# S5 tables on VectorE, the loads of M on GpSimd's queue, and the first q and k weights ahead of the S5 inputs, in a two-layer hybrid trunk

## The chip, the cores and the metric

One core of one Trainium2 chip. The metric is the device time of one execution in microseconds (us). The kernel before took 1287.1 us in the median of three runs (1284.03, 1287.1 and 1289.07).

## What is computed

Two layers over 512 tokens of width 1024, all in float32. Each layer has a mixer and a channel mixer, and both are modulated per sequence by columns that come from a conditioning vector:

```
mod = silu(c) @ mod_w[l] + mod_b[l]            # shift1, scale1, gate1, shift2, scale2, gate2
h = x * (1 + scale1) + shift1
u, q, k, v = split(h @ w_in[l], 512 each)
ssm = s5_mixer(u)       # 32 groups, 16 channels in, 64 complex diagonal states, scan over the tokens, GELU, GLU
att = diff_attention(rotary(q), rotary(k), v)  # 4 heads, two causal softmax maps per head, RMS norm
x = layer_norm(alpha * x + (1 + gate1) * (concat(ssm, att) @ w_out[l]))
h = x * (1 + scale2) + shift2
x = layer_norm(alpha * x + (1 + gate2) * ((silu(h @ w_gate) * (h @ w_up)) @ w_down))
```

## The kernel before

**Products.** Every large product is made as three matmuls in a rounded float32 (mm3, L116): high part by high part, high by low and low by high. A weight tile (wunit) is one 512 KB transfer on SP's queue (wraw, L263), one copy on ScalarE that makes its high part (whi, L113), and one subtraction on VectorE for its low part (wlo, L104). Two wraw buffers and five of each part go round. L101, L104, L107 and L110 are helpers for VectorE (or GpSimd, where `eng` says so), L113 for ScalarE.

**S5.** The 32 groups are worked in four quarters q. For each quarter a layer needs tables. s5_build makes `Gt` and `QT` (two halves each; a half is three products or sums of 128x512: `o = a1*b1`, `ta = a2*b2`, `o = o -/+ ta`, in the inner function cpart), the matrix `kps` on TensorE, its copy `ksb`, and the store of that into a DRAM buffer `kd`. QT goes through TensorE (qps) and becomes Q. s5_rot makes the rotation tables `cs`, from `thl` (two products of 128x256), and stores them into the DRAM buffer `sC`. With these, a quarter runs: inp (UU is copied from u2, the rotation tables come back as `csl`), scan (vps on TensorE, rp and wz on VectorE, with the decay table `dt` that GpSimd writes, L575), and sout (yps from `M` and from Gt). M is eight transfers of 64 KB out of kd. One half of each Gt and QT, and both products of thl, are GpSimd's in the kernel before; the other halves are VectorE's. Layer 0 builds its tables inside its own mixer. Layer 1's are built during layer 0's channel mixer (build_bg), the last two quarters in its down projection, where layer 1's Gt, Q and cs are parked in DRAM.

**S5 inputs.** `us` are the four token blocks of u. s5_u2 spreads each over partitions by four transfers of 64 KB into u2 (16 in all per layer, shown as `u<-us`, L554).

**Order of the work.** After the first stage of layer 0 (u and half of v), the loop over the rest of v and over the q and k products of the four heads calls tick() after each few matmuls. A table of due times (PLAN) says at which tick the next step of the builds, of S5, of attention, of a weight's prefetch ('pf') or of a modulation column ('mod': a 512 KB load `mraw` and one pass of VectorE, L110) is emitted. A scheduler then sets the order inside each engine. Every engine and every DMA queue works its list in that order.

**Attention.** scores, transposed, values for 16 blocks (4 heads of 4), then per head scale (`es` by a power on GpSimd, then `on` = the head's output in PSUM times es, four activations on ScalarE, L791) and output (transposes of on, then `am`).

The end of the down projection's first half needs the gate row G2: it is copied by GpSimd's queue to DRAM and comes back as a broadcast (`G<-gd`), after a one-element copy on GpSimd (`after`, L330) that ties the buffer's reuse to earlier work.

Of the kernel before, what the change touches and what calls it, by code (L numbers as in the profile page):

```python
# [21 lines left out]
PLAN = ({'bld': [1.0733576, 2.9031205, 3.5154466, 12.5034164, 15.1071975, 15.6334384, 16.0575658, 21.8153328, 21.8163328, 22.2319658, 22.2329658, 28.5923397, 30.243001, 33.8382641, 37.0440198, 39.0572108, 39.0582108, 41.3108793, 50.0177884, 51.0998781], 's5': [4.9028951, 13.7411167, 15.9929821, 16.2119172, 16.2129172, 17.6168929, 28.8382807, 31.1407667, 34.4657886, 37.933134, 41.1334701, 41.8351188, 44.9709324, 49.1653528, 55.811875, 56.282631, 56.282731, 74.3701229, 75.0322375, 75.0323375], 'att': [32.001, 32.001001, 32.001002, 32.001003, 32.001004, 32.001005, 32.001006, 32.001007, 37.6865938, 41.7355913, 48.001, 48.2683932, 48.2683942, 48.2683952, 48.2683962, 48.2683972, 48.2683982, 48.617537, 61.3736509, 64.3309693, 65.5921236, 65.5931236, 65.5941236, 65.5941246, 65.5941256, 65.6288754, 65.6288764, 65.6288774, 72.5231302, 73.1266492, 78.0578164, 79.9687438, 81.2657271, 81.530476, 81.5768716, 81.5778716, 82.4637908, 82.4647908, 82.4657908, 83.044295, 83.5736498, 83.5746498, 83.5756498, 85.5723498, 85.6572802, 85.6582802, 85.6592802, 85.9764616, 85.9861658, 89.2215451, 89.674753, 89.674754, 93.4177513, 94.279308, 95.5776624, 99.2190776], 'mod': [13.3492705, 20.2546708, 27.3038673, 31.5542422, 38.8480964, 42.1955201, 43.0984851, 43.8754292, 43.8754302, 48.1035539, 49.3327831, 49.3327841, 49.5166057, 49.5176057, 49.5176067, 49.5176077, 59.8309932, 64.8347651, 77.2024317, 86.1901018], 'pf': [15.228123, 15.3414063, 23.4890323, 23.4900323, 40.4066783, 41.3304558, 48.9949729, 60.7543422, 71.3047183, 78.705196, 86.021538, 89.4349823, 89.827606, 96.6870796], 'cs': [0.6433489, 0.9702106, 4.3739515, 6.5989136]}, {'s5': [0, 13.9288025, 14.9687107, 23.4071258, 23.6099155, 23.9930522, 23.9930532, 23.9930542, 49.9536728, 50.7293131, 50.7303131, 52.6273113, 52.801288, 54.037998, 59.8058402, 63.0448533, 63.0448543, 63.0448553, 76.7900745, 79.030225], 'att': [32.001, 32.001001, 32.001002, 32.001003, 32.001004, 36.5544774, 36.5554774, 49.1404333, 49.1534776, 49.5360247, 49.5370247, 49.5380247, 49.9621102, 50.2217672, 52.4983559, 53.4634231, 53.4644231, 53.4654231, 55.4277196, 58.3250688, 61.5574297, 61.5584297, 61.5594297, 61.5604297, 64.4714996, 64.4715006, 64.4715016, 64.4715026, 64.4715036, 64.4715046, 64.4715056, 64.4715066, 64.4715076, 64.4715086, 64.4715096, 64.4715106, 64.4715116, 64.4715126, 80.4714996, 80.4715006, 80.4715016, 80.4715026, 81.6228446, 85.1505891, 85.1515891, 85.1525891, 87.7329811, 89.4506396, 89.4516396, 89.4526396, 89.4536396, 89.4546396, 92.1036248, 92.1036258, 95.1259822, 99.6815179], 'pf': [1.9638689, 9.1450603, 14.6524633, 14.6534633, 19.8486984, 32.001, 37.8876977, 48.001, 51.1731991, 74.7986995, 80.482311, 90.088235, 93.088235, 96.9]})  # L22
OPT = {'MQ': 'sync', 'MODQ': 'sync', 'q_bld': 1, 'q_s5': 0, 'q_att': 0, 'q_pf': 0, 'CSQ': 'scalar', 'plo': [[1, 0, 1, 0, 0, 0, 0, 0, 0, 0, 0, 0, 0, 0, 0, 0, 0, 0], [0, 0, 0, 0, 0, 0, 1, 1, 1, 0, 0, 0, 0, 1, 0, 0, 0, 0]]}
# [39 lines left out]
def trunk_kernel(tc, xT, x, c, pos, modw, modb, wst, s5a, s5bc, s5d, glub, lamv, subw, lng, lnr, out):  # L63
# [3 lines left out]
    with ExitStack() as es:  # L67
# [344 lines left out]
        def s5_build(l, q, pm):  # L412
# [66 lines left out]
            cpart(qt[:, 1], pwb(0, 1), vb(bbi), pwb(1, 1), vb(bbr), ALU.add, nc.gpsimd)  # L479
            cpart(qt[:, 0], pwb(0, 1), vb(bbr), pwb(1, 1), vb(bbi), ALU.subtract, nc.vector)  # L480
# [17 lines left out]
        def s5_rot(l, q, pm):  # L498

            gs = slice(4 * q, 4 * q + 4)  # L500
            sh = [P, 4, 64]
            bg = lambda v: v[:, gs].rearrange("p (g o) -> p g o", o=1).to_broadcast(sh)
            kb = kio.rearrange("p (o k) -> p o k", o=1).to_broadcast(sh)
            thl = t5([P, 2] + sh[1:], name="thl")
            th, tl = thl[:, 0], thl[:, 1]
            tt(th, kb, bg(pm["hi"]), ALU.mult, eng=nc.gpsimd)
            tt(tl, kb, bg(pm["lo"]), ALU.mult, eng=nc.gpsimd)
            cs = t5([P, 2, 4, 64], name="cs")
            ct, st = cs[:, 0], cs[:, 1]
# [12 lines left out]
            eng.dma_start(sC[q][:, 256:768], cs.rearrange("p r g k -> p (r g k)"))
            eng.dma_start(sC[q][:, 0:256], ns)
# [11 lines left out]
        def s5_load_gm(l, q, src):  # L535
# [8 lines left out]
            MQ = nc.sync if l else getattr(nc, OPT["MQ"])  # L544
            for j in range(8):
                ksrc = kd[l][q, :, 16 * j : 16 * j + 128].rearrange("(g c) x -> c g x", c=16)
                MQ.dma_start(M[16 * j : 16 * j + 16], ksrc)
            return G, M

        def s5_u2(u2, us, t):  # L550
            usv = us.rearrange("p (g2 h x) -> p g2 h x", g2=2, h=2)
            for g2 in range(2):
                for h in range(2):
                    nc.sync.dma_start(u2[h][64 * g2 + 16 * t : 64 * g2 + 16 * t + 16], usv[:, g2, h])  # L554
# [166 lines left out]
        def att_gen(qkts, vt, nlam, gain, mix):  # L721
# [57 lines left out]
            def scale(h):  # L779
# [10 lines left out]
                for i in range(NT):  # L790
                    nc.scalar.activation(on[:, i], po[:, i * P : (i + 1) * P], AF.Copy, scale=es_[:, i : i + 1])  # L791
# [145 lines left out]
        for l in range(L):  # L937
# [7 lines left out]
            if l == 0:  # L945
# [35 lines left out]
                with queued(marks(), (POOL,)), strict():  # L981
# [5 lines left out]
                    for k in range(NK):  # L987
# [11 lines left out]
                        for c_ in START[k]:  # L999
# [12 lines left out]
                            else:  # L1012
                                mods_bg(cols, 2, "A2")
                for t in range(NT):
# [4 lines left out]
                    s5_u2(u2, us[t], t)  # L1019
# [6 lines left out]
            else:  # L1026
                uws = [wunit(wb + kp) for kp in range(4)]
                for t in range(NT):
# [5 lines left out]
                    s5_u2(u2, us[t], t)  # L1034
# [13 lines left out]
            pfs = [*range(8, 18), 20, 18, 19, 21]  # L1048
# [315 lines left out]
```

## Time and profile before

| | |
|---|---|
| median of three runs | 1287.1 us (1284.03 to 1289.07) |
| the profiled execution | 1287.01 us, of which the span is 1285.2 us |
| mean granted TensorE clock of the span | 0.973 |
| busy: TensorE, VectorE, ScalarE, GpSimd | 1190.3, 822.4, 488.4, 201.7 us |
| the chain that ended last, share of the span | TensorE 69%, VectorE 17%, DMA 4%, ScalarE 4%, issue 3%, GpSimd 1% |
| transfers of M (64 KB each) | 64, all on SP's queue |

The span is the stretch that the profiler sees; 1.8 us lie around it. Busy times overlap, since the engines run beside each other, so they don't add up to the span. A stretch is limited by TensorE where TensorE is busy through all of it; where it is not, the question is what it waits for. PE in a row is TensorE, DVE VectorE, ACT ScalarE, POOL GpSimd, SP the engine that only issues transfers; a name with q behind it (SPq) is that engine's DMA queue.

### The profile page before, as it was taken

The numbers are of one execution on the slowest core, as the hardware profiler recorded it, in microseconds if no ns is written. First come the engines' busy times: TensorE is split into PE (matmuls) and PEld (weight loads), VectorE is DVE, ScalarE is ACT, GpSimd is POOL, SyncE is SP. The second block draws the span as 40 slices with busy tenths as digits, with TensorE's granted clock in tenths as the row PEclk, the third lists the DMA queues.
The fourth block names the chain that finished last, engine by engine and source line by source line (L and its number), as shares of the span: only waits on it lengthen the run. The fifth ranks groups of instructions, "written<-read, shape, count | busy, mean of one in ns | idle before, by whom it ended". The sixth has DMA issues, their size and how long they took to land.

```text
span 1285.2 us, 17666 instructions
## 1 busy us (share of the span) xinstructions
PE 1190.3 (93%) x6736; PEld 990.6 (77%) x6736; DVE 822.4 (64%) x1441; ACT 488.4 (38%) x878; POOL 201.7 (16%) x289
## 2 busy tenths in 40 slices
PE   4768889999999999999799999999999999999997
PEld 3557777688888888877587788878888888888885
DVE  6668989866677576698547556775757222235556
ACT  3413447627322222244246245662633222234330
POOL 8833420001002021133000120100000000000001
PEclk9887899999999999989899999999999999999999
DMA  9654337534665666744333554423453333333241
GB/s 357 232 165 115 81 91 238 164 99 150 194 228 183 218 215 191 247 152 148 110 98 99 186 161 123 130 79 102 148 184 111 99 99 99 98 99 113 65 134 66
DMA packets 67638, 188.70 MB, mean 147 GB/s; under 512 B 8064, under 2 KB 22176, under 8 KB 67552
## 3 DMA queue, kind: packets, MB, share of 16 engines
q1 hardware_dynamic: 62352, 175.93, 42.9%
q0 software_dynamic: 3040, 9.22, 2.2%
q10 hardware_dynamic: 2160, 2.41, 0.6%
q8 instruction: 53, 0.87, 0.3%
q14 instruction: 33, 0.27, 0.1%
HBM read 172.90 MB, written 12.53 MB: 144 GB/s over the span
## 4 chain that ended last, share of the span: by engine, by line
PE 69%; DVE 17%; DMA 4%; ACT 4%; issue 3%; POOL 1%; SPq 0%; DVEq 0%; ACTq 0%; POOLq 0%
PE gps L116 37%; PE dps L116 14%; PE ops L116 5%; PE qkps L116 3%; DVE mraw L110 3%; PE vps L116 3%; PE ups L116 2%; DVE wlo L104 2%; DMA wraw<-in_wst 1%; DMA mraw<-in_modw 1%; ACT whi L113 1%; DVE ah L104 1%; PE vps L581 1%; PE po L116 1%; DVE rp L104 1%
## 5 line engine op out<-in xcount | busy, mean ns | idle before, releaser
L104 DVE TENSOR_TENSOR wlo<-wraw,whi 128x1024 fp32r<-128x1024 f32 x180 | 223.9, 1246 | 276.1 <-ACT whi L113 275.8
L113 ACT ACTIVATE whi<-wraw 128x1024 fp32r<-128x1024 f32 x184 | 194.4, 1058 | 374.6 <-PE gps L116 275.7
L116 PE MATMUL gps<-hT2h,whi 128*128 128x512 f32 (+1 forms) x768 | 286.4, 373 | 0.3
L116 PE MATMUL gps<-hT2l,whi 128*128 128x512 f32 (+1 forms) x768 | 285.7, 372 | 0.0
L116 PE MATMUL gps<-hT2h,wlo 128*128 128x512 f32 (+1 forms) x768 | 285.3, 372 | 0.0
L116 PE MATMUL dps<-whi,ah 128*128 128x512 f32 x704 | 223.3, 396 | 11.2 <-DVE rtmp L104 8.1
L116 PEld LDWEIGHTS dps<-whi,ah 128*128 128x128 f32 x704 | 134.0, 191 | 42.1 <-DVE rtmp L104 9.7
L116 PEld LDWEIGHTS gps<-hT2h,whi 128*128 128x128 f32 x768 | 144.6, 188 | 26.0 <-DVE rtmp L104 0.6
L116 PEld LDWEIGHTS gps<-hT2l,whi 128*128 128x128 f32 x768 | 144.6, 188 | 25.2
L116 PEld LDWEIGHTS gps<-hT2h,wlo 128*128 128x128 f32 x768 | 144.6, 188 | 24.7
L116 PE MATMUL dps<-wlo,ah 128*128 128x512 f32 x352 | 138.8, 394 | 0.0
L110 DVE SCALAR_TENSOR_TENSOR mraw<-mraw,scb 128x1024 f32<-128x1024 f32 x96 | 123.3, 1312 | 1.8 <-DMA mraw<-in_modw 1.6
L113 ACT ACTIVATE ah<-aT 128x512 fp32r<-128x512 f32 x88 | 53.8, 627 | 116.9 <-PE dps L116 95.3
L104 DVE TENSOR_TENSOR ah<-aT,ah 128x512 fp32r<-128x512 f32 x88 | 63.0, 727 | 40.0 <-ACT ah L113 39.7
L116 PEld LDWEIGHTS dps<-wlo,ah 128*128 128x128 f32 x352 | 67.2, 191 | 13.7
L116 PE MATMUL qkps<-whi,hTh 128*128 128x256 f32 x128 | 38.9, 307 | 8.3 <-ACT whi L113 8.3
L116 PE MATMUL ops<-whi,am 128*128 128x512 f32 x128 | 44.5, 407 | 0.0
L116 PE MATMUL qkps<-wlo,hTh 128*128 128x256 f32 x128 | 38.9, 304 | 0.5 <-DVE wlo L104 0.5
L753 ACT ACTIVATE e<-sps,nm 128x128 f32<-128x128 f32 (+3 forms) x64 | 33.2, 526 | 15.6 <-DVE nm L751 15.5
L104 POOL TENSOR_TENSOR rs<-rs,mhalf 128x1 f32<-128x1 f32 x16 | 10.8, 676 | 179.7 <-DVE rs L101 179.7
L116 PE MATMUL qkps<-whi,hTl 128*128 128x256 f32 x128 | 38.0, 297 | 0.0
L116 PE MATMUL qkps<-whi,hTnh 128*128 128x256 f32 x128 | 37.4, 293 | 0.0
(290 smaller groups left out, 1914.5 us busy)
## 6 DMA issues: line engine op xcount, KB each, us to landing
wraw<-in_wst SPq DMA_DIRECT2D x184, 512.0 KB, 3.7
mraw<-in_modw SPq DMA_DIRECT2D x96, 512.0 KB, 4.7
M<-kd SPq DMA_DIRECT2D x64, 64.0 KB, 3.4
gb<-in_lnr SPq DMA_DIRECT2D x8, 512.0 KB, 4.1
csl<-sC SPq DMA_DIRECT2D x8, 384.0 KB, 3.1
xT<-in_xT SPq DMA_DIRECT2D x8, 256.0 KB, 7.1
u<-us SPq DMA_DIRECT2D x32, 64.0 KB, 2.5
x<-in_x SPq DMA_DIRECT2D x4, 512.0 KB, 4.4
```

The lines of the kernel that those rows point to most:

```text
L104: (eng or nc.vector).tensor_tensor(out, a, b, op=op)
L110: nc.vector.scalar_tensor_tensor(out, a, s, b, op0=ALU.mult, op1=ALU.mult, accum_out=acc_out)
L113: nc.scalar.activation(out, in_, AF.Copy, scale=scale)
L116: nc.tensor.matmul(ps, a, b, start=start, stop=stop)
L581: nc.tensor.matmul(vps[64 * g2 : 64 * g2 + 64, ri * 256 + 64 * a : ri * 256 + 64 * a + 64], Q[:, a, ri, 64 * g2 : 64 * g2 + 64], U[:, a, 6 ...
L753: nc.scalar.activation(e[:, m, :n], ps[:, m, :n], AF.Exp, bias=nm[:, m : m + 1], accum_out=ss[:, i, m : m + 1])
```

## The change

1. cpart and the two products of thl run on VectorE alone. In each layer these are six operations of 128x512 and two of 128x256 per quarter that leave GpSimd.
2. The eight transfers of M per quarter and layer are issued on GpSimd's queue, no more on SP's.
3. In layer 0, half of the 16 transfers of u2 are issued by ScalarE's queue.
4. In layer 0, the weight tiles 8 and 9 (those of head 0's q and k) are fetched ahead of the copies us and the transfers of u2; the first two 'pf' due times go, and the list of prefetches begins at 10.
5. `on` is made by VectorE (tensor_scalar) and no more by ScalarE.

```diff
-'pf': [15.228123, 15.3414063, 23.4890323, 23.4900323,
...
+'pf': [23.4890323, 23.4900323,
...
-            def cpart(o, a1, b1, a2, b2, op, eng):
+            def cpart(o, a1, b1, a2, b2, op):
 
                 ta = t5(sh, name="ta")
-                tt(m8(o), a1, b1, ALU.mult, eng=eng)
-                tt(ta, a2, b2, ALU.mult, eng=eng)
-                tt(m8(o), m8(o), ta, op, eng=eng)
-
-            cpart(G[:, :, 1], pwb(0, 0), vb(ncim), pwb(1, 0), vb(cre), ALU.subtract, nc.gpsimd)
-            cpart(G[:, :, 0], pwb(0, 0), vb(cre), pwb(1, 0), vb(ncim), ALU.add, nc.vector)
+                tt(m8(o), a1, b1, ALU.mult)
+                tt(ta, a2, b2, ALU.mult)
+                tt(m8(o), m8(o), ta, op)
+
+            cpart(G[:, :, 1], pwb(0, 0), vb(ncim), pwb(1, 0), vb(cre), ALU.subtract)
+            cpart(G[:, :, 0], pwb(0, 0), vb(cre), pwb(1, 0), vb(ncim), ALU.add)
...
-            cpart(qt[:, 1], pwb(0, 1), vb(bbi), pwb(1, 1), vb(bbr), ALU.add, nc.gpsimd)
-            cpart(qt[:, 0], pwb(0, 1), vb(bbr), pwb(1, 1), vb(bbi), ALU.subtract, nc.vector)
+            cpart(qt[:, 1], pwb(0, 1), vb(bbi), pwb(1, 1), vb(bbr), ALU.add)
+            cpart(qt[:, 0], pwb(0, 1), vb(bbr), pwb(1, 1), vb(bbi), ALU.subtract)
...
-            tt(th, kb, bg(pm["hi"]), ALU.mult, eng=nc.gpsimd)
-            tt(tl, kb, bg(pm["lo"]), ALU.mult, eng=nc.gpsimd)
+            tt(th, kb, bg(pm["hi"]), ALU.mult)
+            tt(tl, kb, bg(pm["lo"]), ALU.mult)
...
-            MQ = nc.sync if l else getattr(nc, OPT["MQ"])
             for j in range(8):
...
-                MQ.dma_start(M[16 * j : 16 * j + 16], ksrc)
+                nc.gpsimd.dma_start(M[16 * j : 16 * j + 16], ksrc)
...
-        def s5_u2(u2, us, t):
+        def s5_u2(l, u2, us, t):
...
-                    nc.sync.dma_start(u2[h][64 * g2 + 16 * t : 64 * g2 + 16 * t + 16], usv[:, g2, h])
+                    (nc.scalar if l == 0 and h else nc.sync).dma_start(
+                        u2[h][64 * g2 + 16 * t : 64 * g2 + 16 * t + 16], usv[:, g2, h])
...
-                    nc.scalar.activation(on[:, i], po[:, i * P : (i + 1) * P], AF.Copy, scale=es_[:, i : i + 1])
+                    ts(on[:, i], po[:, i * P : (i + 1) * P], es_[:, i : i + 1], ALU.mult)
...
+                prefetch(wb + 8, wb + 9)
                 for t in range(NT):
...
-                    s5_u2(u2, us[t], t)
+                    s5_u2(l, u2, us[t], t)
...
-            pfs = [*range(8, 18), 20, 18, 19, 21]
+            pfs = [*range(8 if l else 10, 18), 20, 18, 19, 21]
```

Three places where the order of the instructions moves. First SP's queue at the end of layer 0's first stage, before (u_129 and u_130 are the two halves of u2, kd_123 is layer 0's kd, `wraw` is a weight tile):

```order
L554 DMA u_130<-us 16x8x128
L473 DMA kd_123<-ksb 128x128
L651 DMA csl<-sC 128x768
L292 DMA mraw<-in_modw 128x1024
L263 DMA wraw<-in_wst 128x1024
L547 DMA M<-kd_123 16x8x128 x8
L263 DMA wraw<-in_wst 128x1024 x2
```

and the same place of the changed kernel:

```order
L263 DMA wraw<-in_wst 128x1024 x2
L292 DMA mraw<-in_modw 128x1024 x2
L553 DMA u_129<-us 16x8x128 x8
L263 DMA wraw<-in_wst 128x1024 x2
L651 DMA csl<-sC 128x768
L292 DMA mraw<-in_modw 128x1024
L263 DMA wraw<-in_wst 128x1024 x4
L473 DMA kd_123<-ksb 128x128
```

The tiles that stood behind the whole row of u transfers, the first store of kd and a column's load stand ahead of them or right behind the eight that are left; no M is in the row.

Second, GpSimd's list from layer 0's first two quarters on, in the changed kernel (es is attention's, dt and wz are the scan's, gd is the gate row):

```order
L104 TENSOR_TENSOR lve<-ebase,lvs 128x2
L418 DMA s5bc<-in_s5bc 128x256
L546 DMA M<-kd_123 16x8x128 x8
L424 MEMSET s5bc 128x256
L575 COPY dt<-r_361 128x256
L576 MEMSET dt 128x4
L602 MEMSET wz 128x8
L330 COPY M<-u_129 128x1
L546 DMA M<-kd_123 16x8x128 x8
L104 TENSOR_TENSOR es<-es,mhalf 128x4
```

Where the products of Gt, QT and thl stood there are now issues of M, which need the store of kd, and the scan's dt stands behind them.

Third, VectorE's list where the last quarter of layer 1's tables is finished in the down projection, in the changed kernel (ah is the low part of an activation tile):

```order
L107 SCALAR_TENSOR_TENSOR ksb<-mask_86,s5dt,ksb 128x16
L104 TENSOR_TENSOR ta<-pw,s5bc 128x512
L104 TENSOR_TENSOR QT<-QT,ta 128x512
L104 TENSOR_TENSOR wlo<-wraw,whi 128x1024
L104 TENSOR_TENSOR ta<-pw,s5bc 128x512
L104 TENSOR_TENSOR wlo<-wraw,whi 128x1024
L104 TENSOR_TENSOR QT<-QT,ta 128x512
L104 TENSOR_TENSOR ah<-aT,ah 128x512
L104 TENSOR_TENSOR thl<-kio,phihi 128x256
L104 TENSOR_TENSOR thl<-kio,philo 128x256
L101 TENSOR_SCALAR cs<-thl 128x256
```

Before, one ta, one QT and one ah stood between ksb and cs; now both pairs of ta and QT, two wlo and the two products of thl stand there, and the wait for the store of kd is that of the first thl.

## Rows read from the trace of the kernel before

**Rows 1.** Windows: start:end, length, busy of PE, PEld, DVE, ACT, POOL; clock; DMA share, GB/s.

```profile
80.00:100.00 20.00, 5.43 (x60) 4.34 (x59) 11.85 (x19) 2.86 (x6) 9.55 (x14) 0.65 0.40 130
160.00:180.00 20.00, 14.14 (x175) 12.49 (x176) 18.49 (x39) 9.14 (x23) 5.90 (x10) 0.91 0.30 96
540.00:560.00 20.00, 16.98 (x92) 12.92 (x91) 19.84 (x29) 5.22 (x9) 9.07 (x9) 0.83 0.38 133
560.00:580.00 20.00, 20.00 (x94) 16.42 (x93) 19.99 (x40) 9.97 (x16) 6.26 (x8) 1.00 0.50 157
```

**Rows 2.** Chain of 60 to 300 us (layer 0's mixer): start, length, what.

```profile
188.03 2.23 PE qkps L116 x17
...
229.91 1.23 DVE mraw L110 x2
231.17 3.63 DMA mraw<-in_modw
...
267.63 17.05 PE ops L116 x75
```

**Rows 3.** Timeline of SP's queue, 55 to 112 us: start, length, what.

```profile
63.29 16.98 SPq L554 DMA_DIRECT2D u<-us  x15
...
88.00 0.43 SPq L263 DMA_DIRECT2D wraw<-in_wst  x1
90.74 8.93 SPq L547 DMA_DIRECT2D M<-kd  x8
```

**Rows 4.** Waits of PE, 75 to 300 us: for whom, total, times, longest.

```profile
PE qkps L116 <- ACT whi L113: 8.3, 1, 8.3
```

**Rows 5.** Chain of 536 to 640 us (layer 0's channel mixer, down projection).

```profile
540.96 1.70 DVE Gt L104
...
544.85 4.50 DVE mraw L110 x4
...
554.11 2.29 DVE mraw L110 x4
...
557.00 0.60 DVE QT L104
...
573.26 1.80 DVE ah L104
...
579.97 1.36 DVE s5bc L437
...
584.38 2.75 DVE ah L104
587.13 2.24 DVE mraw L110 x2
...
591.24 3.65 DMA wraw<-in_wst
...
610.03 7.02 DMA G<-gd
```

**Rows 6.** Timeline of DVE, 543 to 602 us: an undisturbed copy, and cs.

```profile
543.04 0.46 DVE L437 COPY s5bc<-s5bc 64x128 f32<-64x128 f32 x2
...
601.35 0.29 DVE L101 TENSOR_SCALAR cs<-thl 128x256 f32<-128x256 f32 x1 [2.04 <-DMA kd<-ksb]
```

**Rows 7.** Groups by form, DVE, 60 to 300 us: busy, mean ns, idle before.

```profile
L437 DVE COPY s5bc<-s5bc 64x128 f32<-64x128 f32 x8 | 6.2, 774 | 0.1
...
L104 DVE TENSOR_TENSOR wz<-rp 128x512 f32<-128x512 f32 x4 | 4.6, 1154 | 0.1
```

**Rows 8.** Groups by form, whole span: ht, on and the issue of kd.

```profile
L101 DVE TENSOR_SCALAR ht<-htp,modab 128x128 f32<-128x128 f32 x48 | 18.8, 401 | 4.2 <-PE htp L852 2.3 <-ACT ht L858 1.6
...
L791 ACT ACTIVATE on<-po,es 128x128 f32<-128x128 f32 x32 | 9.1, 368 | 12.6 <-POOL es L104 12.6
...
L473 POOL DMA_DIRECT2D kd<-ksb x4 | 2.4, 596 | 19.9 <-DVE ksb L107 19.9
```

**Rows 9.** DMA issues of the page: form, KB each, median us to landing.

```profile
M<-kd SPq DMA_DIRECT2D x64, 64.0 KB, 3.4
```

More of the change, by code (lines that the diff above doesn't have):

```diff
@@ L23 @@
-OPT = {'MQ': 'sync', 'MODQ': 'sync', 'q_bld': 1, 'q_s5': 0, 'q_att': 0, 'q_pf': 0, 'CSQ': 'scalar', 'plo': [[1, 0, 1, 0, 0, 0, 0, 0, 0, 0, 0, 0, 0, 0, 0, 0, 0, 0], [0, 0, 0, 0, 0, 0, 1, 1, 1, 0, 0, 0, 0, 1, 0, 0, 0, 0]]}
+PLAN = ({'bld': [1.0733576, 2.9031205, 3.5154466, 12.5034164, 15.1071975, 15.6334384, 16.0575658, 21.8153328, 21.8163328, 22.2319658, 22.2329658, 28.5923397, 30.243001, 33.8382641, 37.0440198, 39.0572108, 39.0582108, 41.3108793, 50.0177884, 51.0998781], 's5': [4.9028951, 13.7411167, 15.9929821, 16.2119172, 16.2129172, 17.6168929, 28.8382807, 31.1407667, 34.4657886, 37.933134, 41.1334701, 41.8351188, 44.9709324, 49.1653528, 55.811875, 56.282631, 56.282731, 74.3701229, 75.0322375, 75.0323375], 'att': [32.001, 32.001001, 32.001002, 32.001003, 32.001004, 32.001005, 32.001006, 32.001007, 37.6865938, 41.7355913, 48.001, 48.2683932, 48.2683942, 48.2683952, 48.2683962, 48.2683972, 48.2683982, 48.617537, 61.3736509, 64.3309693, 65.5921236, 65.5931236, 65.5941236, 65.5941246, 65.5941256, 65.6288754, 65.6288764, 65.6288774, 72.5231302, 73.1266492, 78.0578164, 79.9687438, 81.2657271, 81.530476, 81.5768716, 81.5778716, 82.4637908, 82.4647908, 82.4657908, 83.044295, 83.5736498, 83.5746498, 83.5756498, 85.5723498, 85.6572802, 85.6582802, 85.6592802, 85.9764616, 85.9861658, 89.2215451, 89.674753, 89.674754, 93.4177513, 94.279308, 95.5776624, 99.2190776], 'mod': [13.3492705, 20.2546708, 27.3038673, 31.5542422, 38.8480964, 42.1955201, 43.0984851, 43.8754292, 43.8754302, 48.1035539, 49.3327831, 49.3327841, 49.5166057, 49.5176057, 49.5176067, 49.5176077, 59.8309932, 64.8347651, 77.2024317, 86.1901018], 'pf': [23.4890323, 23.4900323, 40.4066783, 41.3304558, 48.9949729, 60.7543422, 71.3047183, 78.705196, 86.021538, 89.4349823, 89.827606, 96.6870796], 'cs': [0.6433489, 0.9702106, 4.3739515, 6.5989136]}, {'s5': [0, 13.9288025, 14.9687107, 23.4071258, 23.6099155, 23.9930522, 23.9930532, 23.9930542, 49.9536728, 50.7293131, 50.7303131, 52.6273113, 52.801288, 54.037998, 59.8058402, 63.0448533, 63.0448543, 63.0448553, 76.7900745, 79.030225], 'att': [32.001, 32.001001, 32.001002, 32.001003, 32.001004, 36.5544774, 36.5554774, 49.1404333, 49.1534776, 49.5360247, 49.5370247, 49.5380247, 49.9621102, 50.2217672, 52.4983559, 53.4634231, 53.4644231, 53.4654231, 55.4277196, 58.3250688, 61.5574297, 61.5584297, 61.5594297, 61.5604297, 64.4714996, 64.4715006, 64.4715016, 64.4715026, 64.4715036, 64.4715046, 64.4715056, 64.4715066, 64.4715076, 64.4715086, 64.4715096, 64.4715106, 64.4715116, 64.4715126, 80.4714996, 80.4715006, 80.4715016, 80.4715026, 81.6228446, 85.1505891, 85.1515891, 85.1525891, 87.7329811, 89.4506396, 89.4516396, 89.4526396, 89.4536396, 89.4546396, 92.1036248, 92.1036258, 95.1259822, 99.6815179], 'pf': [1.9638689, 9.1450603, 14.6524633, 14.6534633, 19.8486984, 32.001, 37.8876977, 48.001, 51.1731991, 74.7986995, 80.482311, 90.088235, 93.088235, 96.9]})
@@ L24 @@
+OPT = {'MODQ': 'sync', 'q_bld': 1, 'q_s5': 0, 'q_att': 0, 'q_pf': 0, 'CSQ': 'scalar', 'plo': [[1, 0, 1, 0, 0, 0, 0, 0, 0, 0, 0, 0, 0, 0, 0, 0, 0, 0], [0, 0, 0, 0, 0, 0, 1, 1, 1, 0, 0, 0, 0, 1, 0, 0, 0, 0]]}
 NOSYNC = mybir.DependencyInfo(mybir.DependencyClass.NoSync, mybir.DependencyReason.DATA)
@@ L1033, in trunk_kernel @@
                     cp(us[t], ps)
-                    s5_u2(u2, us[t], t)
+                    s5_u2(l, u2, us[t], t)
                 vw = []
```

1 line of the change is left out of this document (removed).

## The prediction

> **What bounds the kernel now.** I read the busy times first: TensorE works through 93% of the span, so a gain can only lie where it does not. The view by windows finds those places [rows 1]. From 80 to 100 us TensorE is busy 5.43 of 20 us, and its clock falls to 0.65. From 100 to 240 us it has smaller holes while VectorE is nearly full; the window at 160 us (18.49 of 20) stands for these. From 540 to 580 us VectorE is full (19.84 and 19.99 of 20), and at 540 TensorE loses 3 us. In the gate and up products between these places TensorE is full, so what the change moves there costs and gains nothing.
>
> Then the waits and the queues. The longest single wait of TensorE in layer 0's mixer is for a high part whi, 8.3 us [rows 4]: head 0's second weight tile. Its cause stands in SP's queue [rows 3]. Fifteen transfers of u take 16.98 us to issue (1.13 us each), and the weight is issued only at 88.00, behind them and other entries.
>
> The chain of waits says which of it counts. At 536 to 640 us it runs on VectorE for most of the way, then over a weight's load to the gate row G, which lands 7.02 us after its issue [rows 5]. Near layer 0's mixer end it runs over column loads: a pass of 1.23 us, a load of 3.63 us into the one buffer, a pass again; then 17.05 us of output products [rows 2].
>
> **The sum, down projection of layer 0.** In the chain are operations of VectorE that take longer than their like [rows 5]. A product of 128x512 takes 0.60 us undisturbed (QT at 557.00), two column passes 2.29 (at 554.11), a copy of L437 0.23 [rows 6]. Against these, Gt at 540.96 is 1.1 us too long, the four pieces of mraw at 544.85 2.2, ah at 573.26 1.2, the copy at 579.97 1.1, ah at 584.38 2.15 and mraw at 587.13 1.1. That is 8.9 us, and each lies beside a product of GpSimd; I take it that the two engines hold each other up, and that the 8.9 us go when GpSimd's products go. In their place VectorE gets, before the weight load at 591.24 that carries the chain on, six halves' operations of quarter 2, four of quarter 3 and two products of thl: 10 x 0.60 + 2 x 0.35 = 6.7 us (0.35 is between half of 0.60 and 0.60, for half the size). Net -2.2 us. Behind it the wait for the store of kd stays (2.04 us ahead of cs [rows 6]), but both products of thl now come after it: +0.7. The two more operations on QT hide in that wait; uncovered they would cost 1.2 us. Sum -1.5 us. The far ends are -7.0 us, the whole wait for G, and +7.4 us, if none of the 8.9 comes back. I take **-3 us**: nearer the chain's own sum than -7.0, since the chain holds more such pieces than I listed.
>
> **The sum, mixer of layer 0.** The weights of head 0 no longer stand behind u's transfers. TensorE then has 138 products of q and k ready ahead of the first kps (33, 69 and 36 in its list), at 2.23 / 17 = 0.131 us [rows 2] 18 us of work for a hole of 14.6. So one end is -14.6 us: the hole closes, and nothing else becomes late. The other end comes from VectorE. It gets 24 products of 128x512 and 8 of thl, 17.2 us, and 16 of `on`. Those have no row on VectorE; the bounds are 0.15 us (a quarter of 0.60) and 0.40 (ht, the same size out of PSUM with two operands [rows 8]), and I take 0.30: 4.8 us, 22.0 in all. It has 8.15 idle us in the hole to put them in [rows 1]. What it gets back are at the least eight copies of L437 at 774 instead of 230 ns and four wz at 1154 instead of 600 [rows 7], 6.6 us; 22.0 - 6.6 - 8.15 is +7.2 us. By the ratio of the down projection (8.9 us for two quarters, 17.8 for four) it is 22.0 - 17.8 - 8.15 = -4.0 us. Those are the same operations beside the same products, so I take **-4 us** and keep -14.6 and +7.2 as ends.
>
> Eight of u's transfers go to ScalarE's queue. At SP's 1.13 us an issue, u2 is whole 9 us earlier and ScalarE is held up 9 us at most, at a place where it is mostly idle; the first user of u2 waits for the tables of quarter 0 anyway, so I cost this at nothing. Without that cover it would be worth up to -9 us, which lies inside the end above. The Trainium skill (Trainium Kernel Development and Optimization, Key Constraints) says that queues of several engines share the same DMA engines and that a second one saves only issue time; the trace agrees in so far as issues are what spaces these transfers, and by the rule alone this part would bring those 9 us to u2 and nothing to the time.
>
> **The sum, M and layer 1.** GpSimd pays 0.6 us for the issue of a plain transfer (596 ns [rows 8]), so 8 x 0.6 = 4.8 us per quarter. Behind it stand dt, the zeroing of wz and attention's es. What covers it is that GpSimd has no other work left there, and that M's data, some 3.4 us after an issue [rows 9], are needed only after the scan. SP loses 8.93 us of M in front of weights and columns [rows 3]. In layer 1's mixer TensorE is nearly full, and `on` costs about the same on either engine (368 ns on ScalarE [rows 8]). I take **0**, with ends -3 us (SP free for the columns) and +4.8 us (one quarter's issues uncovered).
>
> The sum is -3 - 4 + 0 = -7 us against the profiled execution's 1287.0 (span 1285.2 and 1.8 around it; the median of the runs is 0.1 above it): **1280.0 us**.
>
> **The rivals.**
> *The hole fills and the end stays.* The mixer's second half hangs on the column loads through one buffer, 4.86 us a round [rows 2]; no part of the change makes these loads shorter. If the first column starts as late as now, the hole's gain turns into waiting there. Then 0 from the mixer and 0 to -3 from the down projection: 1284 to 1287. For it: the chain. Against: SP's queue, which carries the columns too, is rid of M.
> *S5 falls behind.* This one ends slower. In the changed order the scan of quarter 0 stands behind 240 q and k products, before behind 84; 156 x 0.131 is 20.4 us, less the hole of 14.6 it is 5.8 us later, and each later quarter is built by a VectorE that is over 90% full [rows 1] and has 22 us more to do. If it gives back only the 6.6 us named, the mixer ends 7.2 us later by VectorE's sum; with +1 from the down projection 1295. It decides if VectorE is full from 100 us until the last quarter's scan. Against: attention's blocks run earlier for the same reason, so VectorE has less of them later.
> *M comes late.* dt waits behind 4.8 us of issues and M's issues wait for kd's store. If a quarter's scan waits for its dt, the four cost up to 19 us less what is hidden; I count half, on top of the sum: 1289.
> *GpSimd's issues are blocked by VectorE.* Should an issue of M take twice its 0.6 us while VectorE is full, four quarters take 4 x 4.8 = 19 us more of GpSimd's time; uncovered, and with the -7 of the sum, that gives 1299. The one row that bears on it speaks against: the stores of kd were issued at 596 ns in a stretch in which VectorE was 99% busy [rows 1, 8]. The rule is in the Trainium skill (SBUF — State Buffer, Who interferes with whom): a transfer held up by VectorE is one whose descriptors GpSimd writes.
>
> **How the numbers follow.** A measurement of this kernel can tell about 0.5% (6.4 us) from no change. The forecast has 0.50, with a range of its own from 1270 to 1284; the hole filled with the end unmoved has 0.26, M late 0.09, S5 behind 0.11, the blocked issues 0.04. Faster by over 0.5% (below 1280.7): 0.50, which is the forecast, with its upper part made up for by the ends below. Within 0.5%: 0.35, the unmoved end and M late. Slower (above 1293.5): 0.15. The range for 8 in 10 is 1267 to 1294: below it the hole's whole gain with more, above it most of the two slow cases.
>
> **What would show it.** Right, step by step: a window from 80 to 100 us with TensorE busy over 15 us; no wait for whi there; VectorE's column passes at 1.2 us and ah at 0.6 throughout 540 to 600; G landing about 3 us earlier; mean times of L437 near 230 ns. The mixer of layer 0 should end 4 us earlier than now. Wrong: the chain of waits in 100 to 240 us made of VectorE's table products, or dt's copy on GpSimd behind M ahead of a scan, or the operations named too long staying so with GpSimd silent; the last would mean that the 8.9 us have another cause.

## The result, and the profile after

The changed kernel takes **1293.44 us** (median of five, 1290.99 to 1295.04), the kernel before 1285.37 beside it (five runs). The ratio is 1.0055, 95% interval 1.0035 to 1.0075: by that 7.1 us or 0.55% **slower**. The forecast was 1280.0; the time lies inside the range (1267 to 1294) and on the other side of no change.

The profiled spans are 1291.5 and 1285.2 us. Where the 6.3 us lie follows from the starts of gated sums (`rtmp`) on VectorE's timeline. A mixer is taken to end at its fifth one, which the expectations below call the first (the first of all comes 11.5 us earlier, at 273.20 before and 283.77 after, the same 10.6 us later):

| stretch | before, us | after, us | difference | forecast |
|---|---|---|---|---|
| to the end of layer 0's mixer | 284.71 | 295.33 | +10.6 | -4 |
| from there to the down projection's first gated sum | 332.5 | 328.9 | -3.6 | -3 |
| from there to layer 1's mixer end | 279.6 | 279.6 | 0.0 | 0 |
| the rest | 388.4 | 387.7 | -0.7 | 0 |

So one term of the sum is far off, that of layer 0's mixer. The windows of the changed kernel, TensorE's waits, GpSimd's and SP's timelines and the chain tell where it went. First the windows (columns as in [rows 1]):

```profile
80.00:100.00 20.00, 18.27 (x175) 17.69 (x174) 16.54 (x43) 7.25 (x11) 0.73 (x1) 1.00 0.52 173
...
160.00:180.00 20.00, 9.15 (x59) 7.14 (x59) 11.99 (x27) 3.65 (x6) 4.25 (x9) 0.74 0.42 112
180.00:200.00 20.00, 17.38 (x184) 14.49 (x185) 17.95 (x35) 8.74 (x26) 5.65 (x13) 0.83 0.28 77
200.00:220.00 20.00, 15.27 (x158) 13.08 (x158) 16.60 (x40) 8.77 (x23) 1.16 (x2) 0.91 0.41 140
220.00:240.00 20.00, 12.31 (x60) 9.50 (x59) 14.42 (x33) 10.52 (x26) 1.01 (x1) 0.79 0.41 132
```

and three windows of the kernel before that the rows ahead of the prediction do not have:

```profile
180.00:200.00 20.00, 18.56 (x194) 16.11 (x192) 15.00 (x30) 9.51 (x22) 1.16 (x2) 1.00 0.46 149
200.00:220.00 20.00, 19.04 (x152) 17.06 (x151) 18.13 (x35) 15.23 (x38) 1.01 (x1) 1.00 0.73 243
220.00:240.00 20.00, 18.88 (x110) 13.79 (x109) 18.56 (x43) 13.61 (x37) 0.00 (x0) 1.00 0.45 147
```

The hole at 80 us is filled as forecast: TensorE is busy 18.27 us where it was 5.43 [rows 1], a gain of 12.8 us, at full clock. From 160 to 240 us it is given back with more: 9.15 for 14.14, which is 5.0 less, then 1.2, 3.8 and 6.6 us less, 16.5 together, and the granted clock of these windows is 0.74 to 0.91 where it was 0.91 to 1.00. The work that filled the hole was q and k products done earlier; later they are missing as filling while TensorE waits for something else (from 160 to 180 us it runs 59 products where it ran 175). TensorE's three longest waits, 60 to 312 us (for whom, total, times, longest):

```profile
PE yps L621 <- POOL wz L602: 8.1, 1, 8.1
PE po L116 <- DVE am L107: 5.0, 2, 2.8
PE qktp L732 <- DVE qkt L104: 3.7, 1, 3.7
```

The wait for whi [rows 4] is gone. In its place stands one that the kernel before hasn't: 8.1 us for the zeroing of wz, an operation of 0.13 us on GpSimd. GpSimd's timeline says why it is late:

```profile
152.09 0.94 POOL L308 DMA_DIRECT2D gd<-mods  x1
153.04 0.41 POOL L575 COPY dt<-r 128x256 f32<-128x256 f32 x1
153.51 0.10 POOL L576 MEMSET dt<- 128x4 f32 x1
166.78 0.55 POOL L546 DMA_DIRECT2D M<-kd  x1 [13.16 <-DMA kd<-ksb]
167.33 0.13 POOL L602 MEMSET wz<- 128x8 f32 x1
```

The issue of M waits 13.16 us for the store of kd, and wz's zeroing stands behind it in GpSimd's list. What was under way beside that store, the issues of 150 to 170 us tell (form, KB each, median us to landing):

```profile
mraw<-in_modw SPq DMA_DIRECT2D x2, 512.0 KB, 13.1
wraw<-in_wst SPq DMA_DIRECT2D x1, 512.0 KB, 13.0
M<-kd POOLq DMA_DIRECT2D x7, 64.0 KB, 4.8
csl<-sC SPq DMA_DIRECT2D x1, 384.0 KB, 11.1
kd<-ksb SPq DMA_DIRECT2D x1, 64.0 KB, 12.7
gd<-mods POOLq DMA_DIRECT2D x1, 4.0 KB, 10.4
```

Every transfer that was under way with the gate row's store `gd` took 11 to 13 us, kd too, whose four stores on SP's queue have a median of 4.0. (M's seven were issued from 166.78 on, when these had landed.) The store of gd is 4 KB, written as 1024 separate elements. That it is what holds the others is tried in experiment 7.

The other rows that answer to those of before. SP's queue (start, length, what):

```profile
63.72 10.07 SPq L553 DMA_DIRECT2D u<-us  x8
73.88 1.94 SPq L263 DMA_DIRECT2D wraw<-in_wst  x2
```

The groups of VectorE by form, 60 to 300 us:

```profile
L104 DVE TENSOR_TENSOR wz<-rp 128x512 f32<-128x512 f32 x4 | 2.7, 683 | 0.0
L437 DVE COPY s5bc<-s5bc 64x128 f32<-64x128 f32 x8 | 2.0, 250 | 0.1
```

M's issues and `on`, groups by form over the whole span:

```profile
L546 POOL DMA_DIRECT2D M<-kd x64 | 33.8, 535 | 25.6 <-DMA kd<-ksb 23.1 <-issue 2.2 <-POOL M L330 0.3
...
L101 DVE TENSOR_SCALAR on<-po,es 128x128 f32<-128x128 f32 x32 | 9.6, 345 | 6.4 <-POOL es L104 6.4
```

and the page's row of M's transfers:

```profile
M<-kd POOLq DMA_DIRECT2D x64, 64.0 KB, 3.5
```

Eight issues of u in 10.07 us instead of fifteen in 16.98, and weights issued at 73.88 instead of 88.00 [rows 3]. L437 has gone from 774 to 250 ns and the long wz from 1154 to 683 [rows 7]. An issue of M costs GpSimd 0.535 us, and its landing is as before [rows 9]. The chain at the end of the mixer:

```profile
261.19 6.26 DMA mraw<-in_modw
267.47 1.25 DVE mraw L110 x2
268.73 3.36 DMA mraw<-in_modw
272.19 1.23 DVE mraw L110 x2
273.85 1.02 POOL es L104
...
277.19 18.12 PE ops L116 x75
```

As before [rows 2] it runs over column loads into the end, but the 75 output products start at 277.19 instead of 267.63: the last columns and attention's last es, which VectorE feeds behind them, are now what they wait for.

### The profile page after: what moved, and what is told of

It is laid out like the page before. It is cut to its first block, busy times and chain, and to the rows that moved or that the text cites. A ratio compares the mean times of both kernels' runs of the same rounds, so it can differ in the third digit from the quotient of the medians.

```text
span 1291.5 us, 17665 instructions
## 1 busy us (share of the span) xinstructions
PE 1200.4 (93%) x6736; PEld 1000.6 (77%) x6736; DVE 819.9 (63%) x1537; ACT 484.5 (38%) x848; POOL 160.5 (12%) x289
## 4 chain that ended last, share of the span: by engine, by line
PE 68%; DVE 6%; issue 4%; DMA 3%; ACT 2%; POOL 1%; DVEq 0%; SPq 0%; POOLq 0%; ACTq 0%
PE gps L116 37%; PE dps L116 15%; PE ops L116 4%; PE qkps L116 3%; PE glups L116 2%; PE vps L116 1%; PE ups L116 1%; DMA mraw<-in_modw 1%; DVE mraw L110 1%; PE po L116 1%; DMA wraw<-in_wst 1%; DVE wlo L104 1%; PE sps L749 1%; DVE x L107 1%; DVE rtmp L104 1%
## 5 line engine op out<-in xcount | busy, mean ns | idle before, releaser
L104 DVE TENSOR_TENSOR wlo<-wraw,whi 128x1024 fp32r<-128x1024 f32 x180 | 219.9, 1224 | 275.3 <-ACT whi L113 275.0
L110 DVE SCALAR_TENSOR_TENSOR mraw<-mraw,scb 128x1024 f32<-128x1024 f32 x96 | 114.5, 1222 | 8.3 <-DMA mraw<-in_modw 8.2
L104 DVE TENSOR_TENSOR ah<-aT,ah 128x512 fp32r<-128x512 f32 x88 | 60.1, 692 | 43.0 <-ACT ah L113 42.6
L116 PE MATMUL qkps<-whi,hTnl 128*128 128x256 f32 x128 | 37.2, 291 | 0.0
```

What stands on the lines that cost most here:

```text
L104: (eng or nc.vector).tensor_tensor(out, a, b, op=op)
L110: nc.vector.scalar_tensor_tensor(out, a, s, b, op0=ALU.mult, op1=ALU.mult, accum_out=acc_out)
L116: nc.tensor.matmul(ps, a, b, start=start, stop=stop)
```

## The experiments

Twelve kernels, told by what they ask. "rp" is VectorE's first pass of quarter 0's scan, a mark for where S5 stands. Each diff is against the kernel named. Ratios and their intervals are against the kernel before, measured beside each run; differences between two experiments are taken from the ratios. Where a place in the kernel is named, it is read from one trace of each kernel.

**1. Part 1 alone** (against before):

```diff
-            cpart(G[:, :, 1], pwb(0, 0), vb(ncim), pwb(1, 0), vb(cre), ALU.subtract, nc.gpsimd)
+            cpart(G[:, :, 1], pwb(0, 0), vb(ncim), pwb(1, 0), vb(cre), ALU.subtract, nc.vector)
...
-            cpart(qt[:, 1], pwb(0, 1), vb(bbi), pwb(1, 1), vb(bbr), ALU.add, nc.gpsimd)
+            cpart(qt[:, 1], pwb(0, 1), vb(bbi), pwb(1, 1), vb(bbr), ALU.add, nc.vector)
...
-            tt(th, kb, bg(pm["hi"]), ALU.mult, eng=nc.gpsimd)
-            tt(tl, kb, bg(pm["lo"]), ALU.mult, eng=nc.gpsimd)
+            tt(th, kb, bg(pm["hi"]), ALU.mult)
+            tt(tl, kb, bg(pm["lo"]), ALU.mult)
```

> The kernel before with part 1 alone: all table products of S5 on VectorE, in both layers; M, u2, the weights and on as before. If the tables on VectorE are what gains in the down projection, the first rtmp of the down projection comes 3 to 4 us earlier relative to the mixer's end than before. In layer 0's mixer, theory C' (VectorE is the bound there, 17 us more on it) expects an end 3 to 7 us later; the theory that what slows the mixer is GpSimd's queue and the new order of q and k expects an end within 2 us of before, or earlier. Time by the first 1286 to 1290, by the second 1279 to 1284.

1272.73 us, ratio 0.9903 (0.9883 to 0.9923): about 12.5 us faster, below both ranges expected. The mixer of layer 0 ends at 278.52 (-6.2), the next stretch is 6.5 us shorter, layer 1's mixer 2.1. G, which took 7.02 us in the chain [rows 5], shows what became of the down projection:

```profile
565.47 16.35 PE dps L116 x72
...
582.45 11.11 PE dps L116 x48
...
600.09 4.24 DMA G<-gd
```

The chain from 547 to 600 us is now TensorE's own products, no more VectorE's.

**2. Part 1 in layer 1 only** (against 1): `nc.vector if l else nc.gpsimd` in the four places, so that layer 0's tables stay shared.

> The kernel before with part 1 in layer 1 alone; layer 0's tables stay split over VectorE and GpSimd. Theory A (the pieces of VectorE beside GpSimd's products set the down projection): the mixer of layer 0 as before (first rtmp within 1.5 us of 284.7), the down projection 3 to 7 us shorter, time 1277 to 1283. Rival (the whole gain of the tables comes through layer 0's mixer, and the down projection profits from what happened there): less than 2 us gained.

1282.28 us, ratio 0.9966 (0.9951 to 0.9981). Theory A. Layer 0's mixer ends at 285.77, 1.1 us later than before, the stretch behind it is 4.9 us shorter, layer 1's mixer 1.4 longer. So most of the gain on the down projection comes from layer 1's tables, which are built there, and the rest of part 1's gain needs layer 0's. The eight copies L437 of layer 0's mixer take 775 ns here, with GpSimd's products still beside them (774 before), and 216 ns in experiment 1, without them.

**3. Parts 3 and 4** (against before): half of u on ScalarE's queue, weight tiles 8 and 9 ahead of us.

```diff
-                    nc.sync.dma_start(u2[h][64 * g2 + 16 * t : 64 * g2 + 16 * t + 16], usv[:, g2, h])
+                    (nc.scalar if l == 0 and h else nc.sync).dma_start(u2[h][64 * g2 + 16 * t : 64 * g2 + 16 * t + 16], usv[:, g2, h])
...
+                prefetch(wb + 8, wb + 9)
...
-            pfs = [*range(8, 18), 20, 18, 19, 21]
+            pfs = [*range(8 if l else 10, 18), 20, 18, 19, 21]
```

> The kernel before with parts 3 and 4 alone: the first q and k weights ahead of the S5 inputs, and half of these on ScalarE's queue; tables, M and on as before. The theory that putting q, k and attention first makes S5 late (first rp at 128 instead of 113) and with it the mixer's end expects that lateness here too: the first rp 8 us or more later, the end 3 to 10 us later, 1288 to 1297. The theory that this part only fills the hole, and that the rest of the change gives it back, expects a mixer that ends 3 to 10 us earlier, 1277 to 1284.

1301.39 us, ratio 1.0115 (1.0097 to 1.0133): 14.8 us slower, more than the first theory expected. The hole is filled (17.12 of 20 us busy), rp comes at 136.8 instead of 113.0, the mixer ends at 296.69.

**4. Parts 1 and 3** (against 1): only the line of u2 of experiment 3.

> The kernel before with parts 1 and 3: tables on VectorE and half of u2's transfers on ScalarE's queue, with the weights fetched where they were (their issue on SP now stands behind eight transfers instead of sixteen). TensorE's list again has 112 q and k products ahead of the first kps. Theory A (the list order costs, whatever puts it there): the first rp later than 118, and the time 10 us or more above that of the tables alone (1272.7), 1283 to 1295. Theory B (only the prefetch ahead of u2 costs, two queues for u2 gain a little): 1268 to 1274.

1285.15 us, ratio 0.9993 (0.9978 to 1.0009): 11.6 us slower than part 1 alone, theory A's range. Halving SP's row of u lets the weights through at 73.10 by itself (87.61 in experiment 1); rp at 131.7.

**5. Parts 1 and 4** (against 1): the prefetch ahead of us, all of u on SP.

> Before with the table products on VectorE (part 1) and the first q and k weights ahead of us and of u's transfers (part 4), but with all 16 transfers of u on SP's queue and M on SP. Open until now: parts 3 and 4 were only tried together (they cost 15.7 us), and part 3 beside part 1 (it cost 12.4 us against part 1 alone). Theory A: early weights as such make S5 late, by whatever road they come early (theirs are high and low parts that VectorE and ScalarE must make, and q and k products that TensorE then has at hand). Then this kernel has its first rp at 125 us or later, as where u goes on two queues, and takes 1282 to 1290 us. Theory B: it is u's transfers on ScalarE's queue that change the order: in TensorE's list of this kernel the scan of quarter 0 stands behind some 110 q and k products, as with part 1 alone, and not behind 240. Then the first rp comes at 105 to 115 us, the wait for the first weight's high part (8.3 us before) is gone, and the time is 1266 to 1275 us, beside 1272.7 with part 1 alone.

1284.0 us, ratio 0.9998 (0.9985 to 1.001): 12.2 us slower than part 1 alone. rp comes at 114.5, as theory B has it; the time is theory A's. Neither holds whole: the weights cost as much with quarter 0's scan nearly in place. TensorE's waits of 60 to 340 us show one that experiment 1 hasn't, and ScalarE's timeline its reason:

```profile
PE utp L567 <- ACT Q L113: 11.9, 2, 11.2
```

```profile
100.16 0.42 ACT L226 ACTIVATE cs<-thl 128x256 f32<-128x256 f32 x1 [5.76 <-DVE thl L101]
...
106.10 0.42 ACT L226 ACTIVATE cs<-thl 128x256 f32<-128x256 f32 x1 [5.22 <-DVE thl L101]
...
108.19 0.60 ACT L113 ACTIVATE Q<-qps 128x512 f32<-128x512 f32 x1 [1.36 <-DVE cs L101]
```

Q stands behind cs of later quarters in ScalarE's list, and those behind VectorE's work: TensorE, with its q and k products already used up, stands for 11.2 us. In experiment 1 Q stands behind the same two cs (102.91 us), but there the q and k products come only then and fill that time. The windows of 80 to 120 us, experiment 1 first, then this one:

```profile
80.00:100.00 20.00, 6.06 (x61) 4.96 (x61) 14.63 (x38) 3.17 (x6) 1.51 (x5) 0.66 0.49 148
100.00:120.00 20.00, 17.46 (x182) 15.70 (x182) 17.58 (x40) 6.35 (x11) 1.25 (x4) 0.84 0.35 131
```

```profile
80.00:100.00 20.00, 13.03 (x129) 12.25 (x129) 16.25 (x47) 3.91 (x8) 1.91 (x5) 0.94 0.45 128
100.00:120.00 20.00, 8.71 (x93) 6.77 (x93) 16.95 (x40) 6.00 (x11) 0.96 (x3) 0.50 0.33 110
```

TensorE is busy 23.5 us of these 40 in experiment 1 and 21.7 here: the early weights moved the hole, from some 85 to 99 us to some 93 to 109, and did not close it.

**6. S5 held to its place** (against 3): a q or k product of layer 0 may not move ahead in TensorE's list of what was emitted before it.

```diff
+                            pe = nc.tensor.engine
+                            with queued({pe: marks()[pe]} if l == 0 else {}):
```

> The kernel before with parts 3 and 4, and the q and k products of layer 0 held on TensorE in the order in which the program emits them, so that S5's steps of a quarter stand ahead of them again (all of quarter 0's stand ahead of the first product). Same work, weights as early as in the run with parts 3 and 4 alone (1301.4 us). Theory A (what costs is the place of S5's steps in TensorE's list, behind 138 and more products): the first rp comes before 113, the mixer of layer 0 ends 5 us or more earlier than there, time 1275 to 1293. Theory B (what costs is the weights' early transfers, which make u2, kd or the rotation tables late): the first rp stays after 120, and the time near 1300.

1334.52 us, ratio 1.0372 (1.0349 to 1.0395), far outside what any theory gave. rp comes at 123.1 instead of 136.8, but TensorE waits 17.3 us (longest 14.8) for Gt ahead of kps and 11.8 for Q: these are late too, so holding TensorE's list back idles it. The place in the list is part of why quarter 0's scan is late; restoring it gives no time back. Since the edit holds every q and k product of layer 0, it does not say what the place in the list alone costs.

**7. The late gate row** (against the changed kernel): gd is issued where the program has it, not ahead.

```diff
-            G1 = gate_tile(l, 0, late)
+            with queued(marks()):
+                G1 = gate_tile(l, 0, late)
```

> The changed kernel, with one edit: the store of the gate row (gd, on GpSimd's queue) is issued later, behind the work that stands ahead of it in the program; the order on TensorE, VectorE and SP stays the same. Theory A (the 8.1 us wait of TensorE for the zeroing of wz comes from the gate row's store, whose single elements hold the DMA engines while kd's store of quarter 2 waits behind them): kd's store of quarter 2 lands in about 4 us instead of 12.7, the wait for wz falls from 8.1 us to under 1, the mixer of layer 0 ends 5 to 9 us earlier (the first rtmp at about 288 instead of 295.3), and the time is near 1286. Theory B (the kd store is slow for another reason, such as the column and weight loads beside it): the wait stays near 8 us and the time near 1293. Theory C (the wait is real, but the end hangs on column loads that start late anyway): the wait goes, but the first rtmp moves by less than 3 us, and the time is 1291 to 1293.

1286.44 us, ratio 1.0014 (1.0000 to 1.0029): the changed kernel less 7.0, theory A. gd now goes at 227.8 us. In the same window as above the transfers take their usual time, and the wait for wz is gone from TensorE's:

```profile
mraw<-in_modw SPq DMA_DIRECT2D x2, 512.0 KB, 5.5
wraw<-in_wst SPq DMA_DIRECT2D x1, 512.0 KB, 3.5
M<-kd POOLq DMA_DIRECT2D x8, 64.0 KB, 5.3
csl<-sC SPq DMA_DIRECT2D x1, 384.0 KB, 4.6
kd<-ksb SPq DMA_DIRECT2D x1, 64.0 KB, 3.4
```

The mixer ends at 288.79 (-6.5). So gd's store is what held kd, and kd is what held M, wz and TensorE.

**8. wz's zeroing on VectorE** (against the changed kernel): `nc.vector.memset(S[:, :, :, 0:1], 0.0)` for `nc.gpsimd`.

> The changed kernel, with the zeroing of the first scan column (wz) on VectorE instead of GpSimd, so that it no longer stands behind the issue of M for the next quarter. Theory A (GpSimd's queue: wz behind M behind kd's store): TensorE's 8.1 us wait for wz goes, but VectorE still waits some 6 us for the same kd store ahead of a table product, so the mixer gains less than the 8.1, 2 to 6 us, and the time is 1287 to 1291. Theory C (the column loads set the end): no more than 2 us, 1291 to 1294.

1290.35 us, ratio 1.0035 (1.0021 to 1.0049): some 3 us less than the changed kernel's median, but the two intervals overlap, and in its trace the mixer ends no earlier (296.74 for 295.33). So no gain is shown. The wait is renamed, not removed:

```profile
PE yps L621 <- DVE wz L104: 10.4, 2, 7.5
```

VectorE's list has its own wait for the same kd (5.85 us ahead of a table product at 166.26 in the changed kernel). With 7 it follows that the late store matters, not the engine that zeroes.

**9. The load of lv earlier** (against 7): lv, of attention's constants, is fetched by GpSimd's queue in layer 0, since on ScalarE's it stood behind the eight transfers of u (75.2 instead of 67.9).

```diff
-            nc.scalar.dma_start(lv, lamv[l].partition_broadcast(P))
+            (nc.scalar if l else nc.gpsimd).dma_start(lv, lamv[l].partition_broadcast(P))
```

> The run with the gate row later (1286.4 us), with one more edit: attention's small parameter load of layer 0 (lv, 128 KB) goes over GpSimd's queue, no more over ScalarE's, where it stands behind eight transfers of u. VectorE waits for lv at a place ahead of quarter 0's tables. TensorE's list still has some 240 q and k products ahead of quarter 0's scan. Theory A (S5 is late because VectorE's list waits for lv and for the early weights' low parts): Gt of quarter 0 comes 5 us or more earlier, the first rp moves with it to 123 or less, time 1279 to 1284. Theory B (the products ahead of the scan in TensorE's list set it): Gt comes earlier, but the first rp stays within 3 us of 128, and the time within 3 us of 1286.

1290.19 us, ratio 1.0044 (1.0026 to 1.0062): 3.9 us more than 7, the intervals just overlap, and neither theory's range. lv was read 6.6 us earlier (74.08 for 80.68) and quarter 0's Gt came no earlier (96.37 for 94.09); rp moved to 134.6. The suspicion of lv falls.

**10. M on GpSimd, and `on` on VectorE** (against 1): part 2 alone beside part 1; part 5 alone beside part 1; and parts 1, 2 and 5 together, which is the changed kernel without 3 and 4.

> The kernel before with parts 1 and 2: tables on VectorE, M on GpSimd's queue. Theory A (M on GpSimd's queue costs the 4.7 us): 1276 to 1279, with TensorE or VectorE waiting behind GpSimd's issues of M or for a transfer that lands late. Theory B (on costs them): 1271 to 1274.

> The kernel before with parts 1 and 5: tables and on on VectorE. Tables alone took 1272.7 us, tables, on and M on GpSimd's queue 1277.4. Theory A (M on GpSimd's queue costs the 4.7 us): 1270 to 1274. Theory B (on on VectorE costs them): 1276 to 1279.

> The changed kernel without parts 3 and 4: tables and on on VectorE, M on GpSimd's queue; u2 on SP's queue alone, and the first q and k weights where they were. Theory A (parts 3 and 4 make S5 late and cost some 15 us, the rest gains): the first rp is near 110 as with the tables alone, and the time is 1270 to 1278. Theory B (M on GpSimd's queue and on on VectorE cost as well): the time is 1279 to 1288, with a wait of TensorE or VectorE behind an issue of M or behind on.

All three fall into their theory A by time.

| parts | median, us | ratio, interval | mixer of layer 0 ends |
|---|---|---|---|
| 1 and 2 | 1278.62 | 0.9952 (0.9934 to 0.9970) | 279.53 |
| 1 and 5 | **1271.21** | 0.9902 (0.9878 to 0.9925) | 277.00 |
| 1, 2 and 5 | 1277.36 | 0.9932 (0.9913 to 0.9951) | 281.05 |

Part 2 costs: 0.0049 of 1285 is 6.3 us against part 1 alone, with intervals apart. Between the last two rows it is 3.9, with intervals that overlap. Part 5 does nothing that a measurement can tell. Where part 2 costs is not settled. Against part 1 alone, layer 0's mixer ends 1.0 us later and layer 1's is 4.5 us longer (282.1 for 277.6); with part 5 beside it in both kernels, layer 0's ends 4.0 later and layer 1's is only 0.5 longer (276.0 for 275.5). GpSimd's waits of 60 to 300 us in the kernel of parts 1 and 2 have

```profile
POOL M L547 <- DMA kd<-ksb: 22.7, 3, 12.7
```

22.7 us in which nothing behind M runs on GpSimd. The longest of the three is the gate row's store again, which is issued here just ahead of it:

```profile
134.11 0.91 POOL L308 DMA_DIRECT2D gd<-mods  x1 [9.05 <-DVE mods L104]
...
148.28 0.54 POOL L547 DMA_DIRECT2D M<-kd  x1 [12.69 <-DMA kd<-ksb]
```

In the kernel before and in experiment 1 no store of kd is under way with gd (the next one, issued at 140.2 and 139.5 us when gd has landed, takes 3.3 and 3.1 us). So gd may have a part in what M costs; a kernel with M on GpSimd's queue, without parts 3 and 4, and with gd later was not run.

The last row is also the changed kernel without parts 3 and 4, and the most direct test of them: 1.0055 against 0.9932 is 15.8 us that these two parts cost there, and the mixer ends 14.3 us earlier without them. With gd out of the way (experiment 7) they still cost 10.5 us (1.0014 against 0.9932), 7.7 of them up to the mixer's end.

Part 1 alone and parts 1 and 5 can't be told apart; both are faster than the kernel before and the changed one.

## Why the prediction was wrong

**The mixer of layer 0, point by point.** The measured +10.6 us can be followed through a row of kernels, by where the mixer ends: 284.7 before, 277.0 with parts 1 and 5, 281.1 with part 2 as well, 288.8 with parts 3 and 4 and gd later, 295.3 with gd where the changed kernel has it. So the tables and `on` give -7.7, M on GpSimd's queue +4.0, the early weights +7.7 and gd beside kd +6.5. The sizes of the pieces depend on what stands beside them: M costs +1.0 there without part 5, and part 3 or part 4 beside part 1 alone costs +10.4 or +10.1. Only the last step, gd, is one edit to a kernel that is otherwise the same.

**The step that failed** is the mixer's sum, forecast -4 and measured +10.6. It took "-14.6: the hole closes, and nothing else becomes late" as its good end and the excess of VectorE as its other, and put VectorE's extra work into the hole. The early weights stand in it as what closes the hole, never as a cost; the runs show them as a cost of 10 to 12 us (experiments 4, 5 and 10). VectorE's excess, which was to decide between the ends, came back whole (below). And the sum had no term for gd, whose store costs 7.0 us once it is issued beside kd's (experiment 7). A hole that is filled with work from later on is no gain where the end waits for another engine's list; this was the rival of the unmoved end, with 0.26. Even that was too kind: its condition was that the columns start "as late as now", and they start later. Seven traces, with the 7th and the 20th (last) column pass of the mixer on VectorE:

| kernel | rp, us | 7th | 20th | mixer ends |
|---|---|---|---|---|
| before | 113.0 | 180.7 | 257.1 | 284.7 |
| part 1 | 109.1 | 179.7 | 253.6 | 278.5 |
| parts 1, 4 | 114.5 | 186.8 | 264.2 | 288.6 |
| parts 1, 3 | 131.7 | 197.3 | 274.7 | 288.9 |
| parts 3, 4 | 136.8 | 207.0 | 284.9 | 296.7 |
| changed | 128.0 | 199.2 | 277.3 | 295.3 |
| changed, gd later | 128.0 | 190.2 | 272.0 | 288.8 |

The thirteen columns from the 7th to the 20th take 74 to 82 us in each, through one buffer, so a late start comes out at the last pass. With parts 1 and 4 that carries over one to one (+10.6 at the last pass, +10.1 at the end); where S5 is later still, half of it or less does. That other work of TensorE's is done by then would explain it, but is not shown. What is shown is that part 3 and part 4 each cost 12 us beside part 1, that both together cost no more than 16 in any pair of kernels (14.8 against before), and that S5 and the columns are later in all of these. What the two have in common is the weights' early issue on SP's queue; that this is the cause in both is argued from it. In experiments 4 and 5 gd's store also falls beside one of kd (kd lands in 9.1 and 8.0 us there), so some of their 12 us may be gd's. That VectorE and ScalarE work on the freed tiles (1.2 us of wlo each) ahead of S5's tables fits the lists, and experiments 5 and 6 agree with it; it was not isolated, and how much of the cost is the columns and how much waits like Q's stays open. So does why half of u on ScalarE's queue moves quarter 0's scan by 23 us and the prefetch alone by 5.

**u2 on two queues**, "I cost this at nothing": right on u2, wrong on the time. UU is copied at 77.61 and nobody was waiting. But the same edit takes eight entries from in front of the weights on SP's queue, and as a whole it costs 11.6 us (experiment 4). The entries that a moved transfer leaves behind it were counted for M and for the weights, not here.

**M**, "I take 0" with ends -3 and +4.8: 4 to 6 us, at the bad end or beyond it. The rival "M comes late" had the place right, GpSimd's list behind M's issue: there it was dt, in the chip's run wz. Its price was the issues (4.8 us a quarter), and the price that counted was the wait for kd in front of them. The rival of the blocked issues falls: 0.535 us each over all 64.

**The down projection**, -3 forecast, -3.6 measured, but part 1 alone gives -6.5: the far end of -7.0, the whole wait for G, was nearer. The signs named for it are there: passes of 2.29 for two columns and ah at 0.62 to 0.70 us, the copies L437 at 250 ns (0.23 each from 540 to 600 us). That the excess comes from GpSimd's products holds (L437 at 216 ns in experiment 1 and 775 in experiment 2). With 96 operations more (64 of the tables, 32 `on`) VectorE's busy total fell from 822.4 to 819.9 us, so over the kernel all of the added time came back. With part 1 alone it fell from 181.5 to 178.7 us between 60 us and the end of layer 0's mixer, with 31 operations more: there too all came back, where the pessimistic end counted 6.6 us and the forecast 17.8 of 22.0. The Trainium skill (SBUF — State Buffer, Who interferes with whom) states that an instruction of VectorE with two inputs in SBUF contends with one of GpSimd that reads SBUF; these traces agree (the long wz, a sum of two such inputs, 1154 ns before and 683 after).

**The rival S5 falls behind**, 0.11 and 1295, is the one that came nearest in time. Its reason, VectorE with 22 us more to do, is refuted: part 1 makes S5 earlier (109.1), and VectorE, which was to be full until the last quarter's scan, is busy 11.99 of 20 us from 160 us on. Its other reason, q and k products ahead of S5, is what the runs support in part. That the time came near its 1295 is luck: gd's 7.0 us, which no rival had, are in it.

## What to carry to other kernels

A hole in the busiest engine filled with work that is due later anyway is worth nothing until the end of the stage moves: look first at what the stage's last wait hangs on and ask whether the filling delays that. Here the filling moved the hole (experiment 5). A transfer's issue sits in an in-order list, so before it is moved to another engine, ask what it waits for and what small thing stands behind it there; and a transfer taken off a queue lets the next ones through earlier, which is an edit too. Test the parts of a bundle one by one: here one part gave 12.5 us and the rest took back 19.5 (1.0055 against 0.9903).

## What the runs showed of the hardware

A store of 4 KB as 1024 separate elements took 10.4 us, and 512 KB loads issued beside it 13 us; with that store moved away, loads at the same place took 3.5 to 5.5. In most of that time (155.5 to 164.5 us) the DMA engines were busy for 58% and moved 29 GB/s; from 80 to 100 us of the same kernel they were busy for 52% and moved 173. And the mutual hold-up of VectorE and GpSimd was larger than I had taken it for: 64 table products and 32 `on` more on VectorE, and VectorE was busy 2.5 us less.
